# Down-projection of a gated MLP by seven block products: operand sums on VectorE, kept in DRAM, the last product by pairs of row blocks

## The chip, the core and the metric

The kernel runs on one core of one Trainium2 chip. The metric is device time in microseconds (us) of one execution, smaller is better. The median of three runs before the change is 3221.31 us (3219.59 to 3222.55).

## The reference

One layer of a streaming encoder on x of 2048 tokens by 1024 channels, all in 32-bit floats: a token-mixing sublayer, a layer norm, then a gated MLP with a causal convolution, and a second layer norm. What the change touches is the end of it:

```python
def conv_ffn(x, conv_w, conv_b, w_up, w_down):
    h = x @ w_up                                   # 2048 x 1024 by 1024 x 5632
    h = depthwise causal conv, width 3 (h) + conv_b
    gate, val = jnp.split(h, 2, axis=-1)
    return (jax.nn.silu(gate) * val) @ w_down      # 2048 x 2816 by 2816 x 1024
...
x = layer_norm(ALPHA * x + ffn(x), ln2_g, ln2_b)
```

## The kernel before

Every 32-bit product is made of three matrix products of operands split in two: `split` writes the rounded part of a tile with ScalarE (ACT) and the rest, source minus rounded part, with VectorE (DVE); `mm3` issues the three matmuls of 128 by 512 outputs. Both projections of the MLP are done by a seven-product block scheme (two halves in each of the three sizes), so that seven products of half-size blocks replace eight; the price is sums of blocks of the operands and of the results.

**Up-projection** (`ffn_up`, L1714). A loop over 44 steps i (22 pairs of feature columns for the first half of the tokens, then 22 for the second, in reverse) and seven products k in each. A product is 12 matmuls into one PSUM bank of four; `after` adds it into the tiles `pre` on DVE. One step behind, `conv` applies the convolution (ACT, and two DVE operations for each of two parts), the SiLU (ACT) and the product of the two parts, one 128x1024 multiply on GpSimd (POOL); then follows the store `h<-b` into DRAM, issued by SyncE (SP, L1758). `slot_back` (L1656 to L1660) issues the loads `b<-wk` of the split weights of the second half, one per product, also on SP.

**Weight sums for the down-projection** (`down_sums`, L1847), run beside the second half of the up-projection as a background job. For each of 11 row blocks c of w_down it loads a 128x1024 tile `xraw` (one buffer) and two 128x512 tiles `xtmp` (four buffers), makes four differences with `sub`, each 128x512 and on POOL, and stores four tiles `wt` into DRAM (L1874 to L1881).

**Down-projection** (`Down`, L245, and `ffn_down`, L1885). Seven products p in the order 0, 4, 3, 5, 2, 6, 1. The first six have 11 steps c; a step multiplies one token tile (128 features by 1024 tokens, eight row blocks of 128) with one 128x512 weight tile: 8 x 3 = 24 matmuls, into eight PSUM banks, four of which are halves of two two-bank tiles. For each step ahead of the matmuls, `Down.load` (three steps ahead) issues the loads on SP, `Down.sum` (two steps ahead) makes the token sum on POOL for the products 4, 3, 5 and 6 (128x1024, add or subtract) and keeps those of 4 and 3 in DRAM (`hs`), and `Down.split` (one step ahead) splits tokens and weights. After the last step of a product, `after` moves each row block's bank into the result tiles R0 and R1 with ACT (products 0 and 4) or DVE, and makes two more sums of results on POOL. Product 1 goes in three passes over the 11 steps, of four, two and two row blocks, with the split weights kept.

**Last layer norm.** When product 2 is done, the eight row blocks of R1 are final and are queued for `norm_stages`, kind "AP": sums of the rows on ACT, a power on POOL, small operations on DVE, the scale on ACT, the gain on POOL and the shift on DVE. The blocks of R0 follow in product 1 with gain and shift folded into two DVE operations of 128x1024. The residual x is added by `residual`, one DVE operation of 128x1024 for each block, in products 2 (R1) and 6 (R0). `turn` runs after each step and issues stores two steps after they were asked for, on SP's queue.

The order of instructions on each engine is made when the kernel is built, by a scheduler that takes what is ready, first come first; each engine and SP's queue then keep that order. An instruction that waits holds everything behind it on its engine.

Of the kernel before, what the change touches and what calls it, by code (L numbers as in the profile page):

```python
# [15 lines left out]
OP = mybir.AluOpType  # L16
# [228 lines left out]
class Down:  # L245
# [4 lines left out]

    def __init__(self, k):
        self.k, self.half = k, NF // 2
        self.seq = [(p, c, 0, 8) for p in (0, 4, 3, 5, 2, 6) for c in range(self.half)]
        self.seq += [(1, c, a, b) for a, b in ((0, 4), (4, 6), (6, 8)) for c in range(self.half)]
        self.raw, self.ready, self.kept = {}, {}, {}

    def sources(self, p, c):
# [3 lines left out]
        tokens = {0: (h(0, 0),), 4: (h(1, 0), h(1, 1)), 3: (k.d_hs[0][c], h(0, 0)), 5: (h(0, 0), h(1, 0)),  # L261
                  2: (h(1, 1),), 6: (h(0, 1), k.d_hs[1][c]), 1: (h(0, 1),)}[p]
# [7 lines left out]
    def load(self, j):  # L270
        if j >= len(self.seq):
            return
        p, c, a, b = self.seq[j]
        nc = self.k.nc
        tokens, weights = self.sources(p, c)
        x = []
        for d in tokens:
            t = self.k.T([P, (b - a) * P])
            nc.sync.dma_start(t, d[:, a * P:b * P])
            x.append(t)  # L280
        w = None
# [3 lines left out]
        self.raw[j] = x, w  # L285

    def sum(self, j):

        if j >= len(self.seq):
            return  # L290
        p, c = self.seq[j][:2]
        x = self.raw[j][0]
        if len(x) == 2:
            self.k.nc.gpsimd.tensor_tensor(x[0], x[0], x[1], op=OP.add if p == 4 else OP.subtract)
            x.pop()
        if p in (3, 4):
            self.k.store(self.k.d_hs[0 if p == 4 else 1][c], x[0])

    def split(self, j):
        if j >= len(self.seq):  # L300
            return
        p, c, a, b = self.seq[j]
# [8 lines left out]
        self.ready[j] = v, self.k.split_new(x)  # L311

# [4 lines left out]
class Kern:  # L317
# [156 lines left out]
    def setup(self):  # L474
# [27 lines left out]
        self.d_hs = [[self.DT([P, 2 * G], name="hs") for _ in range(NF // 2)] for _ in range(2)]  # L502
# [1211 lines left out]
    def ffn_up(self):  # L1714
# [54 lines left out]
        for i in range(2 * NF):  # L1769
# [30 lines left out]
            for k in range(7):  # L1800
# [46 lines left out]
    def down_sums(self):  # L1847
# [5 lines left out]
        sub = lambda out, x, y: nc.gpsimd.tensor_tensor(out, x, y, op=OP.subtract)  # L1853
# [31 lines left out]
    def ffn_down(self):  # L1885
# [6 lines left out]
        def norm(b, y, kind):  # L1892
            def gen():
                act = kind[0] == "A"
                gain, shift = (nc.gpsimd, nc.vector) if kind[1] == "P" else (None, None)
                yield from self.norm_stages(y, gb, act, gain, shift, self.out[0, b * P:(b + 1) * P, :])
# [15 lines left out]

        def after(k, i, ps):
# [4 lines left out]
            add = nc.vector.tensor_tensor  # L1918
# [140 lines left out]
```

## Time and profile before

| | us |
|---|---|
| median of 3 runs | 3221.31 |
| the profiled execution, its own time | 3227.53 |
| its span (first to last instruction) | 3225.7 |
| outside the span | 1.8 |
| TensorE busy | 3053.4 (95%) |
| VectorE busy | 2474.6 (77%) |
| ScalarE busy | 1595.9 (49%) |
| GpSimd busy | 876.1 (27%) |

Mean granted clock of TensorE is 0.979 of full speed. Names in rows: PE is TensorE (PEld its weight loads), DVE VectorE, ACT ScalarE, POOL GpSimd, SPq the queue of SyncE, which issues nearly all DMAs. A row of a timeline has the start, the time it took, the engine, the operation, output and inputs by tile names (`p` PSUM, `b` a 4 KB tile of the large pool, `m` a 2 KB tile), and in brackets how long the engine stood idle before it and what ended that. Most instructions stand under one line, L133, since a helper records them; they are told apart by tiles.

### The profile page before, as it was taken

Reading aid. Unit: us, or ns where it says so; the run is one execution under the profiler, and the core shown is the slowest. Engines: PE = TensorE matmul, PEld = TensorE weight load, DVE = VectorE, ACT = ScalarE, POOL = GpSimd, SP = SyncE. Lnnn points to the kernel's source line nnn. Section 1 sums busy time; section 2 is a strip of 40 time slices with the busy share of each in tenths; the row PEclk is TensorE's granted clock in tenths of the full one; section 3 lists DMA queues with packets and bytes.
Section 4 is the critical chain, followed back from the end, with each engine's and each line's share of the span. In section 5 each row is a group of like instructions: output and inputs, shape, how many; then the busy total and the mean of one; then the engine's idle time right before and its main releaser. Section 6 shows DMA issues by size and latency. Waiting matters only on the chain. (4 is left out here: it accounts for less than half of the span.)

```text
span 3225.7 us, 44051 instructions
## 1 busy us (share of the span) xinstructions
PE 3053.4 (95%) x14750; PEld 2542.7 (79%) x14750; DVE 2474.6 (77%) x4622; ACT 1595.9 (49%) x3048; POOL 876.1 (27%) x704
## 2 busy tenths in 40 slices
PE   8988899999999999599999999999999999999978
PEld 8886688888888788488787878888777788888866
DVE  5589987987799989988775688999954555568775
ACT  3365746874578777577611244444522322333253
POOL 2017510010010221001222234555433111355441
PEclk9999899999999999899999999999999999999989
DMA  7657784765377332221454777888877766778762
GB/s 251 236 183 279 252 319 150 264 220 200 129 261 256 116 103 66 67 96 53 144 202 173 239 277 287 297 297 294 306 271 290 284 221 216 279 259 339 257 214 90
DMA packets 321089, 704.36 MB, mean 218 GB/s; under 512 B 26906, under 2 KB 128990, under 8 KB 320862
## 3 DMA queue, kind: packets, MB, share of 16 engines
q1 hardware_dynamic: 312222, 685.80, 60.3%
q10 hardware_dynamic: 8640, 15.73, 1.3%
q8 instruction: 117, 1.92, 0.2%
q14 instruction: 110, 0.90, 0.1%
HBM read 449.09 MB, written 252.35 MB: 217 GB/s over the span
## 5 line engine op out<-in xcount | busy, mean ns | idle before, releaser
L133 PE MATMUL p<-b,b 128*128 128x512 f32 (+3 forms) x12568 | 2834.4, 382 | 126.4 <-DVE b L133 53.5
L133 PEld LDWEIGHTS p<-b,b 128*128 128x128 f32 x12568 | 2260.8, 190 | 572.1 <-DVE b L133 55.8
L133 POOL TENSOR_TENSOR b<-b,b 128x1024 f32<-128x1024 f32 (+4 forms) x154 | 386.8, 2516 | 454.3 <-DVE b L133 254.5
L133 ACT ACTIVATE b<-p 128x512 fp32r<-128x512 f32 (+11 forms) x634 | 360.2, 603 | 300.1 <-PE p L133 289.8
L133 DVE TENSOR_TENSOR b<-p,b 128x512 f32<-128x512 f32 (+3 forms) x614 | 388.1, 654 | 139.1 <-PE p L133 93.2
L133 ACT ACTIVATE m<-b,F 128x448 bf16<-128x448 f32 (+3 forms) x448 | 366.2, 820 | 87.1 <-DVE F L133 69.5
L133 ACT ACTIVATE b<-b 128x512 fp32r<-128x512 f32 (+3 forms) x299 | 236.0, 807 | 343.9 <-DVE b L133 118.8
L133 DVE TENSOR_SCALAR_CACHE_REDUCE m<-b,F 128x512 bf16<-128x512 f32 (+6 forms) x476 | 370.1, 808 | 2.4 <-DMA gm<-m 1.6
L133 DVE SCALAR_TENSOR_TENSOR b<-b,cw,b 128x1023 f32<-128x1023 f32 (+1 forms) x176 | 249.2, 1425 | 136.1 <-ACT b L133 135.3
L133 DVE TENSOR_TENSOR b<-b,b 128x1024 fp32r<-128x1024 f32 (+6 forms) x221 | 283.5, 1292 | 56.5 <-ACT b L133 39.3
L133 ACT ACTIVATE b<-m 128x512 fp32r<-128x512 f32 x215 | 133.0, 627 | 285.2 <-DVE m L133 125.0
L133 DVE TENSOR_TENSOR b<-m,b 128x512 fp32r<-128x512 f32 x215 | 203.1, 953 | 83.9 <-ACT b L133 83.7
L133 ACT ACTIVATE b<-b,cw 128x1024 f32<-128x1024 f32 x88 | 107.8, 1238 | 300.0 <-DVE b L133 209.0
L133 ACT ACTIVATE b<-b,mx 128x1024 f32<-128x1024 f32 (+2 forms) x192 | 171.6, 896 | 74.2 <-DVE mx L133 72.4
L133 PE MATMUL p<-ident,b 128*128 128x128 f32 x1248 | 194.9, 275 | 9.5 <-DVE b L133 7.2
L133 DVE SCALAR_TENSOR_TENSOR b<-b,ws,b 128x768 f32<-128x768 f32 (+5 forms) x154 | 154.8, 1034 | 51.6 <-ACT b L133 49.4
L133 DVE CUSTOM_DVE_ANT_0 b<-p,b 128x1024 f32<-128x1024 f32 (+2 forms) x192 | 173.6, 906 | 21.1 <-PE p L133 20.2
L133 PEld LDWEIGHTS p<-ident,b 128*128 128x128 f32 x1248 | 152.8, 141 | 43.0 <-DVE b L133 4.9
L133 PE MATMUL p<-kst,b 128*128 128x384 f32 (+3 forms) x656 | 152.8, 365 | 6.8 <-DVE b L133 4.7
L133 POOL TENSOR_SCALAR b<-b 128x1024 fp32r<-128x1024 f32 (+2 forms) x50 | 53.3, 1069 | 350.3 <-DMA b<-in_w_in_dram 175.2
L133 ACT ACTIVATE m<-p 128x512 f32<-128x512 f32 (+2 forms) x172 | 100.8, 586 | 76.6 <-PE p L133 71.0
L133 PEld LDWEIGHTS p<-kst,b 128*128 128x128 f32 x656 | 114.3, 193 | 28.5 <-ACT b L133 13.5
(127 smaller groups left out, 1663.6 us busy)
## 6 DMA issues: line engine op xcount, KB each, us to landing
b<-wk SPq DMA_DIRECT2D x339, 512.0 KB
wk<-b SPq DMA_DIRECT2D x211, 512.0 KB
b<-h SPq DMA_DIRECT2D x88, 512.0 KB
b<-in_w_ffn_up_dram SPq DMA_DIRECT2D x44, 512.0 KB
h<-b SPq DMA_DIRECT2D x44, 512.0 KB
b<-vv SPq DMA_DIRECT2D x80, 256.0 KB
xT<-b SPq DMA_DIRECT2D x32, 512.0 KB
b<-xT SPq DMA_DIRECT2D x32, 512.0 KB
```

What stands on the lines that cost most here:

```text
L133: return f(*args, **kw)
```

## The change

Token sums: the sum for product 4 is made during product 0 (and the first two steps of 4), spread by the table `early`, and stored in `hs`; product 4 loads it, and makes the sum for product 3 from it in `split`; product 3 makes the one for product 6; each is stored in DRAM. Products 4 and 3 walk their steps in reverse. Only product 5 still sums in `sum`. All these sums, `sub` of `down_sums` and the result sums are on DVE (`nc.vector`). Loads run four steps ahead, sums three, splits two. All norms take the form with gain and shift on DVE; residuals of both halves are added in product 2. Product 1 goes in four passes of two row blocks; the matmuls of row block 7 are held back and issued after all others.

```diff
         self.seq = [(p, c, 0, 8) for p in (0, 4, 3, 5, 2, 6) for c in range(self.half)]
-        self.seq += [(1, c, a, b) for a, b in ((0, 4), (4, 6), (6, 8)) for c in range(self.half)]
+        self.seq += [(1, c, a, a + 2) for a in range(0, 8, 2) for c in range(self.half)]
+        self.early = {n * 4 // 3: self.half - 1 - n for n in range(self.half)}
+    def step(self, j):
+        p, c, a, b = self.seq[j]
+        return p, self.half - 1 - c if p in (3, 4) else c, a, b
...
-        tokens = {0: (h(0, 0),), 4: (h(1, 0), h(1, 1)), 3: (k.d_hs[0][c], h(0, 0)), 5: (h(0, 0), h(1, 0)),
-                  2: (h(1, 1),), 6: (h(0, 1), k.d_hs[1][c]), 1: (h(0, 1),)}[p]
+        tokens = {0: (h(0, 0),), 4: (k.d_hs[0][c],), 3: (k.d_hs[1][c],), 5: (h(0, 0), h(1, 0)), 2: (h(1, 1),),
+                  6: (k.d_hs[2][c],), 1: (h(0, 1),)}[p]
...
+        e = self.early.get(j)
+        side = []
+        if e is not None:
+            side += [get(self.k.d_h[1][e], 0, 8), get(self.k.d_h[1][half + e], 0, 8)]
+        if p == 4:
+            side.append(get(self.k.d_h[0][c]))
+        elif p == 3:
+            side.append(get(self.k.d_h[0][half + c]))
...
     def sum(self, j):
         if len(x) == 2:
-            self.k.nc.gpsimd.tensor_tensor(x[0], x[0], x[1], op=OP.add if p == 4 else OP.subtract)
+            self.k.nc.vector.tensor_tensor(x[0], x[0], x[1], op=OP.subtract)
             x.pop()
-        if p in (3, 4):
-            self.k.store(self.k.d_hs[0 if p == 4 else 1][c], x[0])
...
     def split(self, j):
         self.ready[j] = v, self.k.split_new(x)
+        side = self.side.pop(j, ())
+        add = self.k.nc.vector.tensor_tensor
+        if len(side) > 1:
+            t = side[0]
+            add(t, t, side[1], op=OP.add)
+            self.k.store(self.k.d_hs[0][self.early[j]], t)
+        if p == 4:
+            t = side[-1]
+            add(t, x, t, op=OP.subtract)
+            self.k.store(self.k.d_hs[1][c], t)
+        elif p == 3:
+            t = side[-1]
+            add(t, t, x, op=OP.subtract)
+            self.k.store(self.k.d_hs[2][c], t)
...
-                    if 2 <= k < 5:
-                        down.load(k - 2)
-                    if k == 6:
-                        down.split(0)
+                    if 1 <= k < 5:
+                        down.load(k - 1)
+                    if k > 4:
+                        down.split(k - 5)
...
-        sub = lambda out, x, y: nc.gpsimd.tensor_tensor(out, x, y, op=OP.subtract)
+        sub = lambda out, x, y: nc.vector.tensor_tensor(out, x, y, op=OP.subtract)
...
             elif k == 4:
-                nc.gpsimd.tensor_tensor(R0[i][:, hi], R0[i][:, lo], R1[i][:, lo], op=OP.add)
+                add(R0[i][:, hi], ps, R0[i][:, lo], op=OP.add)
...
-                nc.gpsimd.tensor_tensor(R1[i][:, lo], R1[i][:, hi], R1[i][:, lo], op=OP.subtract)
...
-                queue.append(norm(8 + i, R1[i], "AP"))
+                queue.append(norm(8 + i, R1[i], True))
...
-                elif b0 == 0:
-                    banks = {i: self.PS1() for i in range(4)}
                 else:
-                    t = self.PS2()
-                    banks = {b0: t[:, lo], b0 + 1: t[:, hi]}
+                    banks = {i: self.PS1() for i in range(b0, b1)}
...
-            down.load(j + 3)
-            down.sum(j + 2)
-            down.split(j + 1)
+            down.load(j + 4)
+            down.sum(j + 3)
+            down.split(j + 2)
...
+            if k == 2:
+                if 1 <= c < 9:
+                    load_residual(c - 1)
+                    load_residual(8 + c - 1)
+                if c < 4:
+                    for i in (2 * c, 2 * c + 1):
+                        add(R1[i][:, lo], R1[i][:, hi], R1[i][:, lo], op=OP.subtract)
+                if c >= 3:
+                    residual(c - 3, R0[c - 3])
+                    residual(8 + c - 3, R1[c - 3])
...
+            for i in range(b0, b1):
+                if i == 7 and k == 1:
+                    last.append((i, c, w, xh, xl))
+                else:
+                    pair(i, c, w, xh, xl)
-            norm_tick(k == 1 and (b0 or c % 2 == 0) or c % 2 == 1)
+            norm_tick(k != 1 or c % 3 == 0)
+        for args in last:
+            pair(*args)
```

## Rows read from the trace of the kernel before

**Rows 1.** Waits of PE from 3040 us to the end: total us, times, longest.

```profile
PE p L133 <- DVE b L133: 25.3, 5, 21.5
```

**Rows 2.** Timeline of PE, end of the down-projection.

```profile
3062.01 59.67 PE L133 MATMUL p<-b,b 128*128 128x512 f32 x262 [0.44 <-DVE b L133]
3143.16 51.23 PE L133 MATMUL p<-b,b 128*128 128x512 f32 x215 [21.48 <-DVE b L133]
...
3213.39 0.98 PE L133 MATMUL p<-b,b 128*128 128x512 f32 x3 [0.78 <-DVE b L133]
```

**Rows 3.** Timeline of DVE in products 2 and 6: splits, and evictions (b<-p).

```profile
3060.12 1.23 DVE L133 TENSOR_TENSOR b<-b,b 128x1024 fp32r<-128x1024 f32 x1 [0.58 <-ACT b L133]
3061.27 4.91 DVE L133 TENSOR_TENSOR b<-p,b 128x512 f32<-128x512 f32 x8
...
3095.15 2.48 DVE L133 TENSOR_TENSOR b<-m,b 128x512 fp32r<-128x512 f32 x1 [0.75 <-ACT b L133]
...
3108.56 0.68 DVE L133 TENSOR_TENSOR b<-m,b 128x512 fp32r<-128x512 f32 x1
...
3142.43 1.87 DVE L133 TENSOR_TENSOR b<-p,b 128x512 f32<-128x512 f32 x3
```

**Rows 4.** Windows: length; busy PE, PEld, DVE, ACT, POOL; PEclk; DMA share; GB/s.

```profile
3061.00:3122.00 61.00, 60.23 (x265) 49.25 (x263) 49.34 (x72) 33.90 (x51) 30.50 (x16) 1.00 0.70 235
...
3143.00:3148.00 5.00, 4.84 (x12) 3.83 (x13) 3.28 (x6) 0.63 (x1) 0.00 (x0) 0.51 0.48 146
```

**Rows 5.** Groups by form from 2780 us to the end: count, busy us, mean ns, idle before.

```profile
L133 POOL TENSOR_TENSOR b<-b,b 128x1024 f32<-128x1024 f32 x53 | 151.4, 2861 | 129.4 <-DMA b<-h 59.0 <-PE p L133 22.1 <-DVE b L133 17.8
...
L133 DVE SCALAR_TENSOR_TENSOR b<-b,b 128x1024 f32<-128x1024 f32 x16 | 24.5, 1539 | 6.4 <-DMA b<-x 6.3
...
L133 DVE TENSOR_TENSOR b<-b,b 128x256 fp32r<-128x256 f32 x22 | 8.9, 421 | 18.1 <-ACT b L133 15.6 <-PE p L133 2.3 <-issue 0.2
```

**Rows 6.** Windows of the up-projection, columns as in rows 4.

```profile
2450.00:2500.00 50.00, 46.31 (x203) 37.63 (x203) 19.70 (x24) 12.63 (x21) 20.44 (x14) 1.00 0.75 274
2500.00:2550.00 50.00, 43.99 (x192) 35.50 (x191) 27.52 (x33) 15.85 (x29) 12.26 (x7) 1.00 0.84 310
```

**Rows 7.** Timeline of POOL there: first weight differences of two blocks, the multiply between.

```profile
2447.97 1.29 POOL L133 TENSOR_TENSOR xtmp<-xraw 128x512 f32<-128x512 f32 x1 [14.18 <-DMA xraw<-in_w_ffn_down_dram]
...
2453.19 2.40 POOL L133 TENSOR_TENSOR b<-b,b 128x1024 f32<-128x1024 f32 x1
2469.19 1.30 POOL L133 TENSOR_TENSOR xtmp<-xraw 128x512 f32<-128x512 f32 x1 [13.60 <-DMA xraw<-in_w_ffn_down_dram]
```

**Rows 8.** SP's queue: its waits from 2340 to 2780 us, then its timeline.

```profile
SPq L1758 <- POOL b L133: 157.7, 22, 11.2
...
2455.62 0.32 SPq L1758 DMA_DIRECT2D h<-b  x1
...
2461.11 0.55 SPq L1860 DMA_DIRECT2D xraw<-in_w_ffn_down_dram  x1
```

**Rows 9.** Timeline of ACT: first eviction of product 0, and of product 4.

```profile
2819.55 0.60 ACT L133 ACTIVATE b<-p 128x512 f32<-128x512 f32 x1 [18.84 <-PE p L133]
...
2879.66 0.60 ACT L133 ACTIVATE b<-p 128x512 f32<-128x512 f32 x1 [26.30 <-PE p L133]
```

**Rows 10.** Timeline of DVE in product 1: first and fourth of four norms in a row.

```profile
3180.49 1.28 DVE L133 SCALAR_TENSOR_TENSOR b<-b,nm,b 128x1024 f32<-128x1024 f32 x1
...
3192.28 1.28 DVE L133 SCALAR_TENSOR_TENSOR b<-b,nm,b 128x1024 f32<-128x1024 f32 x1
```

**Rows 11.** A window with the DMA engines full, columns as in rows 4.

```profile
2900.00:2950.00 50.00, 50.00 (x222) 41.09 (x221) 39.16 (x28) 18.75 (x24) 32.91 (x13) 1.00 1.00 396
```

**Rows 12.** Timeline of DVE in an up-projection step without weight differences.

```profile
2604.00 0.69 DVE L133 TENSOR_TENSOR b<-p,m 128x512 f32<-128x512 f32 x1 [0.84 <-PE p L133]
...
2615.96 2.60 DVE L133 SCALAR_TENSOR_TENSOR b<-b,cw,b 128x1023 f32<-128x1023 f32 x2 [3.11 <-ACT b L133]
```

**Rows 13.** Timeline of DVE: its last instruction.

```profile
3220.68 1.28 DVE L133 SCALAR_TENSOR_TENSOR b<-b,nr,b 128x1024 f32<-128x1024 f32 x1
```

More of the change, by code (lines that the diff above doesn't have):

```diff
@@ L272, in load, with get @@
             return
-        p, c, a, b = self.seq[j]
-        nc = self.k.nc
-        tokens, weights = self.sources(p, c)
[L276 to L281, printed above, removed]
+        p, c, a, b = self.step(j)
+        nc, half = self.k.nc, self.half
+        def get(d, x=a, y=b):
+            t = self.k.T([P, (y - x) * P])
+            nc.sync.dma_start(t, d[:, x * P:y * P])
+            return t
+        tokens, weights = self.sources(p, c)
+        x, w = [get(d) for d in tokens], None
         if a == 0:
@@ L285, in load @@
         self.raw[j] = x, w
+        e = self.early.get(j)
[6 more added lines that the diff above has]
+            side.append(get(self.k.d_h[0][half + c]))
+        if side:
+            self.side[j] = side
     def sum(self, j):
@@ L301, in split @@
             return
-        p, c, a, b = self.seq[j]
+        p, c, a, b = self.step(j)
         (x,), w = self.raw.pop(j)
@@ L501, in setup @@
         self.d_wt = [[self.DT([P, 512], name="wt") for _ in range(NF // 2)] for _ in range(4)]
-        self.d_hs = [[self.DT([P, 2 * G], name="hs") for _ in range(NF // 2)] for _ in range(2)]
+        self.d_hs = [[self.DT([P, 2 * G], name="hs") for _ in range(NF // 2)] for _ in range(3)]
         self.I = {}
@@ L1890, in ffn_down, with norm @@
         queue, norming, gb, xs = [], [], None, {}
-        def norm(b, y, kind):
+        def norm(b, y, act):
             def gen():
-                act = kind[0] == "A"
-                gain, shift = (nc.gpsimd, nc.vector) if kind[1] == "P" else (None, None)
-                yield from self.norm_stages(y, gb, act, gain, shift, self.out[0, b * P:(b + 1) * P, :])
+                yield from self.norm_stages(y, gb, act, None, None, self.out[0, b * P:(b + 1) * P, :])
             return gen()
@@ L1911, in residual @@
             nc.vector.scalar_tensor_tensor(y, xs.pop(b), ALPHA, y, op0=OP.mult, op1=OP.add)
+        add = nc.vector.tensor_tensor
         def after(k, i, ps):
-            add = nc.vector.tensor_tensor
             if k == 0:
@@ L1929, in after @@
                 add(R1[i][:, hi], ps, R0[i][:, hi], op=OP.add)
-                nc.gpsimd.tensor_tensor(R1[i][:, lo], R1[i][:, hi], R1[i][:, lo], op=OP.subtract)
             elif k == 2:
                 add(R1[i][:, lo], ps, R1[i][:, lo], op=OP.add)
-                queue.append(norm(8 + i, R1[i], "AP"))
+                queue.append(norm(8 + i, R1[i], True))
                 R1[i] = None
-            elif k == 6:
-                add(R0[i][:, hi], ps, R0[i][:, hi], op=OP.add)
             else:
                 add(R0[i][:, lo], ps, R0[i][:, lo], op=OP.add)
-                queue.append(norm(i, R0[i], "D-" if i >= 6 else "A-"))
+                queue.append(norm(i, R0[i], i < 6))
                 R0[i] = None
+        last = []
         for j, (k, c, b0, b1) in enumerate(down.seq):
             if c == 0:
-                banks = {}
                 if k != 1:
```

17 lines of the change are left out of this document (6 added, 11 removed).

## The prediction, made before the changed kernel was run

> **What bounds the kernel now.** I read the page first: PE is busy 95% of the span, so a gain has to come from the other 5% or from the end. The waits of PE in the last 190 us name DVE for 25.3 us, 21.5 of it in one piece [rows 1]. The timeline of PE shows where: product 6 runs without a gap, then PE stands for 21.48 us [rows 2]. It resumes at 3143.16, and the first eviction of product 6 on DVE runs from 3142.43 to 3143.11 [rows 3]: row blocks 0 and 1 share a two-bank PSUM tile, so block 1's last matmuls wait for block 0's eviction, and that eviction stood in DVE's queue behind 21 us of other work. DVE was busy 49.34 of 61 us in product 6 [rows 4], but many of its instructions were long: the 128x512 split remainder takes 0.68 us alone, and 2.48 us where a POOL operation runs beside it [rows 3]; POOL's 128x1024 operations take 2.86 us each, 53 of them in this stretch [rows 5]. After the stall the clock was granted at 0.51, the lower of its two levels (1.2 of 2.4 GHz), for 5 us, in which 12 matmuls ran [rows 4]. Then I looked for other gaps. Only the up-projection has some: 3.69 and 6.01 us in two windows of 50 us, 9.7 in all [rows 6]. There POOL stands 14 us for the load `xraw` before its first weight difference, and the multiply, ready long before, stands behind it [rows 7]; SP's store `h<-b` waits for that multiply (157.7 us in 22 waits), and the next `xraw` load stands behind the store, 5.5 us later [rows 8]. This ring takes 21.2 us (2447.97 to 2469.19 [rows 7]). A step of the up-projection needs 7 x 12 matmuls; one matmul takes 0.2277 us (60.11 us between the first evictions of products 0 and 4, 264 matmuls [rows 9]), so 19.1 us. The ring is 2.1 us slower than PE, and once the slack is gone PE loses that much a step.
>
> **The change, part by part.** PE's work stays: seven products of 264 matmuls.
>
> *Work taken off POOL in the down-projection.* POOL keeps only the small power. Product 6's DVE work then is: 8 evictions of 0.61 us [rows 3] 4.9; 11 splits of 0.68 + 1.23 [rows 3] 21.0; 8 norms of 3.5 us each (three norms with three 128x256 splits take 11.79 us [rows 10], a split 0.42 [rows 5]) 28.1. That is 54.0 of 60.1 us. It fits, so the eviction that ended the long stall comes in time: **-21.5 us**, and the slow clock goes with it: 5 us hold 22 matmuls at full clock and held 12, **-2.3**. The other waits of rows 1 come to 25.3 - 21.5 = **-3.8**.
>
> *What DVE takes over before that.* Token sums, 33 x 1.23 = 41 us over four products, at most 1.23 to 2.5 a step beside 1.91 of splits, in steps of 5.46 us; evictions in product 4 and result differences, 16 x 0.69. Product 2 is the fullest: splits 21.0, evictions 4.9, differences 5.4, 16 residuals of 1.28 (the like operation in rows 10) to 1.54 [rows 5], 20.5 to 24.6, together 52 to 56 of 60.1. All this lies beside PE, with splits now two steps (10.9 us) ahead; if that cover goes, DVE bounds (rival B). At the ends of five products PE meets DVE's queue; the one such wait of before that shows its size is 0.44 us [rows 2]: bounds 0 and, were DVE a 128x1024 operation and an eviction late, 1.9; I take 0.44 x 5 = **+2.2**, since DVE is less loaded than there.
>
> *Loads, stores and SP.* Per c one load and one store of 512 KB more, 22 DMAs, at 0.32 to 0.55 us of SP each [rows 8], hidden in 360 us. Product 0 is the tightest: 7 steps' own loads, 4 steps of product 4's, 8 pairs for the sums and 8 or 9 stores are 23.6 MB in 60.1 us, 393 GB/s. The trace has 396 GB/s with the DMA engines full and PE without a gap [rows 11], so I take nothing; loads lead by four steps, 21.8 us.
> The Trainium skill's "DMA: Bandwidth & Descriptors" (section "Where 436 GB/s comes from") says that for transfers between HBM and SBUF about 358 GB/s bind. Rows 11 go against it, on a core alone; by it, product 0 would need 66 us, late by 6.
>
> *Weight differences on DVE.* 44 x 0.68 = 30 us, in a stretch where DVE was busy 19.7 to 27.5 of 50 us [rows 6]. What matters is the ring. In a step, DVE works without a gap through convolution and first evictions, and only then idles: 0.84 us before the eviction at 2604.00, 3.11 before the next convolution [rows 12]. The scheduler gives an engine to what is ready, first come first, and the differences come later in the code; so I expect them in those gaps, behind the convolution. POOL's multiply and the store `h<-b` are then no longer behind a difference, and the ring is open: **-9.7**. Bounds: 0 if the ring closes through DVE, and worse if DVE waits long (rivals A and C).
>
> *Product 1.* Steps of 6 matmuls, 1.37 us. DVE needs 0.68 + 0.42 = 1.1 us of splits in the first pass. In a later pass of 15.0 us it needs 11 x 0.42, two norms of 3.5 and two evictions of 0.69: 13.0. In the last, block 6 alone takes 7.5 us of PE, and DVE's 13.0 less the 2.7 us of lead stick out by 2.8; block 7 then runs from splits long made. I take **+4** for the passes; bounds 0 and, if each of the six norms holds up the splits by its own 3.5 us less 2.7 of lead, 5 more than the 2.8.
>
> *The end.* From the last matmul's end, 3214.37 [rows 2], to the span's end 11.3 us: 7.6 of DVE with two norms mixed [rows 13], then 3.7 for the store. With block 6 done before, one norm is left: an eviction, two operations of 1.28, small ones and the power's wait; bounds 5 and 7.6, I take 6.2: **-1.4**.
>
> The sum: -21.5 - 2.3 - 3.8 - 9.7 - 1.4 + 2.2 + 4 = **-32.5**. The profiled execution took 3227.5, so 3195.0 for one like it. The median of the runs, 3221.3, lies 6.2 below it; if part of that is the profile's own cost and part lay in the stalls that go, half of it, 3, stays: 3192, so I forecast **3191**, with 3184 to 3199 of its own.
>
> **Rivals.**
> A, *the ring closes again through DVE*: if differences stand ahead of the convolution in DVE's queue, landing, one or two differences, the convolution's second part with evictions, the multiply and the 5.5 us of SP make about 21 us as before. Against it: rows 12. For it: POOL's order of before put them ahead of the multiply [rows 7]. The 9.7 us stay: **3201**.
> B, *DVE becomes the bound*: 54 of 60.1 us leaves 10%; each split also waits for ACT, 0.58 to 0.75 us [rows 3], twice in a step: 11 x 1.3 = 14 us in products 2 and 6 each, which then need 66 to 70. The lead of 10.9 us takes most; 6 us of each stick out: **3203**. The norms' 3.5 us hold their waits already, which speaks against it. The Trainium skill's "Perfetto Trace Analysis" (section "Optimizing Scalar/DVE Operations") says that if DVE is saturated, moving some work to GPSIMD may make sense, while noting that the two share a port; this change goes the other way. By the first half of that rule product 6 gets slower, and this rival is it; rows 3, 2.48 against 0.68 us, side with the second half.
> C, *slower: DVE waits for the weight rows*. The loads `xraw` keep POOL standing 13.6 to 14.2 us [rows 7]. Should DVE stand as long for each of 11 blocks, evictions stop: PE has four banks, about three products or 8.2 us, and loses 6 us a block, some 8 times, while the ring stays: 3191 + 9.7 + 48 = **3249**. It decides for slower from about 3.4 us lost in each of 11 blocks. Against it: DVE's queue has 10 us of other work in a step, which POOL had not.
> D, *the change does not reach its end in product 0*: at the DMA limit, loads come late beyond the lead; 330 GB/s instead of 393 would put them 11 us back, half the lead, so it shows only as a few us at the next ends: **3195**.
>
> **How the numbers follow.** Chances: the forecast 0.52, A 0.16, B 0.14, D 0.04, C 0.14, of which 0.05 are mild cases that eat just the gain. The range reaches from 3178 (all stalls gone, no price in product 1, the whole 6.2 us) to 3213 (A and B together); it leaves out C. A measurement here can tell 0.2%, 6.4 us, from no change. Faster by more: 0.86 less 0.01 for an A and B that add up with a price of product 1, 0.85; within it 0.05; slower 0.10.
>
> **What the profile would show.** Right: no gap of PE over 2 us at the end of product 6, clock 1.00 there; 128x512 split remainders at 0.68 us; the windows of rows 6 at 50 of 50; SP's wait of L1758 near nothing; one norm after the last matmul. Wrong: PE waits named DVE in the up-projection, or `DMA xraw` as what DVE waited for (A, C); DVE without a gap in products 2 and 6 with PE waiting at their ends (B); DMA full and PE waiting in product 0 or 4 (D).

## The result, and the profile after

The median after the change is 3177.57 us (3175.19 to 3179.14, four runs), against 3221.93 (3219.59 to 3222.62) before, where a fourth run has joined the three ahead of the prediction: a ratio of 0.9859, interval [0.9847, 0.9871], 44.4 us faster. The forecast was 3191 with a range from 3178: the direction was right and the main mechanism in part, the size was too small, and the median lies 0.4 us under the range. The profiled execution took 3178.85 us (span 3177.1, mean granted clock 0.986 against 0.979). Line numbers of the kernel after are 29 higher in the parts quoted: L1787 is the store `h<-b`.

To see where the 48.6 us between the two spans lie, I cut each at two places. The first is the start of the last eight transposes of operands, which stand before anything that the change touches; the timelines of PE have them, first before, then after:

```profile
2243.49 1.03 PE L133 MATMUL p<-ident,xraw 128*128 128x128 f32 x8
```

```profile
2238.74 1.03 PE L133 MATMUL p<-ident,xraw 128*128 128x128 f32 x8
```

So 4.7 us were won before the change could act; over twenty profiles of kernels alike up to there the place moves between 2231.4 and 2244.8. The second cut is the first eviction of product 0 on ACT, before in [rows 9], here in the timeline of ACT after:

```profile
2798.11 0.60 ACT L133 ACTIVATE b<-p 128x512 f32<-128x512 f32 x1 [9.84 <-PE p L133]
```

**Stretch A**, between the cuts (the second half of the up-projection), went from 576.1 to 559.4: -16.7. **Stretch B**, from there to the span's end, from 406.2 to 378.9: -27.3 (to the first eviction of product 2 nothing, 241.7 against 241.5; the rest lies behind it).

Stretch B first. The timeline of PE after (columns as in rows 2):

```profile
2801.94 60.25 PE L133 MATMUL p<-b,b 128*128 128x512 f32 x264 [0.69 <-ACT b L133]
2863.60 291.17 PE L133 MATMUL p<-b,b 128*128 128x512 f32 x1281 [1.41 <-DVE b L133]
3156.19 0.73 PE L133 MATMUL p<-b,b 128*128 128x512 f32 x2 [1.41 <-ACT b L133]
3157.28 3.15 PE L133 MATMUL p<-b,b 128*128 128x512 f32 x11 [0.36 <-DVE nt L133]
3161.32 6.87 PE L133 MATMUL p<-b,b 128*128 128x512 f32 x29 [0.89 <-DVE nt L133]
```

From 2863.60 PE runs 291 us without a stop: the 21.48 us of [rows 2] are gone. The waits of PE after, from 3020 us to the end (columns as in rows 1):

```profile
PE p L133 <- ACT b L133: 1.4, 1, 1.4
PE p L133 <- DVE nt L133: 1.3, 2, 0.9
```

Of the 25.3 us that PE waited for `DVE b` there [rows 1] no row is left. The windows after (columns as in rows 4; the product windows reach over parts of products 0, 4, 2 and 6):

```profile
2250.00:2300.00 50.00, 47.97 (x209) 38.57 (x208) 45.97 (x55) 19.95 (x33) 22.16 (x12) 1.00 0.84 298
2300.00:2350.00 50.00, 45.81 (x191) 36.52 (x190) 47.24 (x64) 27.73 (x47) 4.79 (x2) 0.97 0.80 276
2350.00:2400.00 50.00, 50.00 (x222) 41.40 (x221) 36.38 (x43) 12.81 (x24) 7.18 (x3) 1.00 0.93 334
2450.00:2500.00 50.00, 50.00 (x222) 41.42 (x221) 32.24 (x41) 13.95 (x24) 6.68 (x3) 1.00 0.91 320
2500.00:2550.00 50.00, 50.00 (x223) 41.39 (x222) 31.56 (x39) 13.98 (x27) 7.21 (x3) 1.00 0.78 284
2741.00:2798.00 57.00, 57.00 (x253) 47.19 (x252) 42.19 (x41) 20.70 (x29) 2.70 (x1) 1.00 1.03 411
2798.00:2858.00 60.00, 59.31 (x262) 48.53 (x261) 35.03 (x36) 21.29 (x30) 0.00 (x0) 1.00 1.00 403
2980.00:3040.00 60.00, 60.00 (x266) 49.44 (x265) 48.98 (x56) 17.86 (x22) 0.00 (x0) 1.00 0.69 246
3040.00:3100.00 60.00, 60.00 (x266) 49.40 (x265) 46.23 (x93) 35.45 (x62) 9.21 (x8) 1.00 0.58 188
```

The two windows of [rows 6] now hold 50.00 of 50 us of PE. But stretch A gained more than these two windows had lost. Windows before, for a part of it that the prediction had not looked at:

```profile
2250.00:2300.00 50.00, 46.58 (x197) 37.74 (x197) 45.56 (x47) 20.31 (x32) 30.58 (x17) 0.97 0.81 289
2300.00:2350.00 50.00, 43.34 (x181) 34.51 (x180) 45.91 (x58) 25.66 (x43) 17.77 (x10) 0.96 0.80 283
2350.00:2400.00 50.00, 50.00 (x217) 41.26 (x216) 28.27 (x35) 17.10 (x30) 17.29 (x11) 0.97 0.82 288
```

The granted clock is 0.97, 0.96 and 0.97 here, so for some of the time it was at the lower of its two levels. The timeline of PE before, in the same part:

```profile
2261.78 19.34 PE L133 MATMUL p<-b,b 128*128 128x512 f32 x84 [0.91 <-DVE b L133]
2283.63 34.84 PE L133 MATMUL p<-b,b 128*128 128x512 f32 x144 [2.51 <-DVE b L133]
2319.68 3.01 PE L133 MATMUL p<-b,b 128*128 128x512 f32 x12 [1.21 <-DVE b L133]
2325.74 20.71 PE L133 MATMUL p<-b,b 128*128 128x512 f32 x84 [3.05 <-DVE b L133]
2348.84 1.76 PE L133 MATMUL p<-b,b 128*128 128x512 f32 x4 [2.39 <-DVE b L133]
```

Five waits for DVE, 10.07 us, and by the windows some 0.10 x 50 = 5 us of clock. After, the same part has waits of 0.97, 0.98, 0.40, 1.70 and 1.96, 6.01 us, and 0.03 x 50 = 1.5 us of clock. That is 9.7 (ring) + 4.1 (gaps) + 3.5 (clock) = 17.3, against 16.7 measured.

### The profile page after: what moved, and what is told of

Read it like the earlier page. It is cut to its first block, busy times and chain, and to the rows that moved or that the text cites. A ratio compares the mean times of both kernels' runs of the same rounds, so it can differ in the third digit from the quotient of the medians.

```text
span 3177.1 us, 44106 instructions
## 1 busy us (share of the span) xinstructions
PE 3042.5 (96%) x14750; PEld 2534.0 (80%) x14750; DVE 2486.0 (78%) x4737; ACT 1587.3 (50%) x3051; POOL 644.4 (20%) x592
## 5 line engine op out<-in xcount | busy, mean ns | idle before, releaser
L133 DVE TENSOR_TENSOR b<-b,b 128x1024 fp32r<-128x1024 f32 (+6 forms) x268 | 302.9, 1141 | 76.0 <-DMA b<-h 29.9
L133 POOL TENSOR_TENSOR b<-b,b 128x1024 f32<-128x1024 f32 (+3 forms) x94 | 226.8, 2415 | 493.1 <-DVE b L133 339.8
L133 DVE TENSOR_TENSOR b<-m,b 128x512 fp32r<-128x512 f32 x215 | 151.2, 711 | 49.0 <-ACT b L133 48.8
```

What stands on the lines that cost most here:

```text
L133: return f(*args, **kw)
```

## The experiments

Each kernel was timed beside the kernel before on one chip, and its ratio is to that; the medians of before were 3224.1, 3223.2, 3227.4, 3219.9 and 3222.0 in the five groups (3221.9 beside after itself), so ratios compare across groups and medians do not. Stretches A and B of each profile:

| kernel | ratio, 95% | A | B |
|---|---|---|---|
| before | 1 | 576.1 | 406.2 |
| b_again | one run | 576.9 | 408.4 |
| b_diff_dve | 0.9942 [0.9929, 0.9954] | 557.1 | 406.8 |
| b_hstore | 1.0001 [0.9992, 1.001] | 581.3 | 405.5 |
| b_sum_dve | 0.9985 [0.9975, 0.9995] | 578.3 | 400.0 |
| b_norm_dve | 0.9957 [0.9943, 0.997] | 576.1 | 392.1 |
| b_norm_res | 0.9947 [0.9931, 0.9964] | 576.9 | 392.6 |
| b_min | 0.9897 [0.9882, 0.9911] | 558.6 | 391.9 |
| b_min_sum | 0.9866 [0.9848, 0.9884] | 557.3 | 381.3 |
| after | 0.9859 [0.9847, 0.9871] | 559.4 | 378.9 |
| a_diff_pool | 0.9923 [0.991, 0.9937] | 577.2 | 379.4 |
| a_sum_pool | 0.9868 [0.9853, 0.9883] | 559.2 | 378.8 |
| a_split1 | 0.9871 [0.9855, 0.9887] | 562.5 | 379.0 |
| a_norm_pool | 0.9875 [0.9858, 0.9893] | 559.2 | 385.1 |
| a_p1_old | 0.9863 [0.9847, 0.9879] | 558.6 | 383.0 |
| a_p1_old2 | 0.9876 [0.9859, 0.9893] | 559.5 | 383.4 |
| a_again | 0.9859 [0.9844, 0.9873] | 558.7 | 379.2 |
| best1 | 0.9849 [0.983, 0.9869] | 557.8 | 378.3 |
| best2 | 0.9852 [0.983, 0.9874] | 557.2 | 377.3 |
| a_again2 | 0.9858 [0.984, 0.9877] | 558.8 | 378.7 |

### The weight differences

b_diff_dve is before with one line changed, a_diff_pool is after with it undone, and b_again is before, unchanged:

```diff
-        sub = lambda out, x, y: nc.gpsimd.tensor_tensor(out, x, y, op=OP.subtract)
+        sub = lambda out, x, y: nc.vector.tensor_tensor(out, x, y, op=OP.subtract)
```

> The kernel before with one edit: the weight differences of the down-projection on VectorE. Between the two profiles the up-projection's second half and the step into it gained 16.7 us (first eviction of product 0 came 21.4 us earlier, the last transposes before it 4.7 us earlier). Theory 1: all of that comes from this edit, 9.7 us from the ring through POOL's queue (gaps in the windows 2450 to 2550 go) and the rest from DVE no longer slowed by POOL between 2261 and 2349 us: 3205 us. Theory 2: the differences only account for the ring, the rest comes from elsewhere in the change: 3212 us.

> The changed kernel with the weight differences back on POOL, all else as changed. Theory 1: it gives back what they brought, 16.7 us: 3194 us, with PE gaps of 1.3 to 2.5 us a step again in the windows 2450 to 2550. Theory 2: it gives back the ring alone, 9.7 us: 3187 us.

> The kernel before once more, for a second profile of it. The first took 6.2 us more than the median, and stood 4.7 us behind the changed kernel's before the first instruction that the change touches. If that is chance of one execution, this one stands elsewhere (3219 to 3223 us, and the same place earlier by some us); if the profile costs it, it repeats (3227 us).

b_diff_dve took 3205.93 us (3201.09 to 3209.09), 18.2 under before, as theory 1 had it: the line alone is the whole gain of stretch A, and stretch B with its long stall stays. From 2342 us to 2780, where the window ends, its timeline of PE has no gap, so the gaps of [rows 6] are gone too:

```profile
2342.19 438.17 PE L133 MATMUL p<-b,b 128*128 128x512 f32 x1932 [0.56 <-DVE b L133]
```

a_diff_pool took 3199.03 (3195.1 to 3202.27), and A goes back to 577.2. That is theory 1's direction, 5 us above its 3194; the stretches account for 18.3 us of the difference to after, and the rest is within the intervals of the two ratios. b_again (3231.86, one run) came out above both of its expectations, with the transposes at 2244.81; it repeats both stretches of before within 2.2 us. What the line does to DVE between 2250 and 2350 us, by groups by form (columns as in rows 5), before and then in b_diff_dve:

```profile
L133 DVE SCALAR_TENSOR_TENSOR b<-b,cw,b 128x1022 f32<-128x1022 f32 x10 | 15.2, 1524 | 0.1
...
L133 DVE TENSOR_TENSOR b<-p,b 128x512 f32<-128x512 f32 x20 | 13.1, 678 | 0.0
L133 DVE TENSOR_TENSOR b<-m,b 128x512 fp32r<-128x512 f32 x12 | 11.8, 999 | 1.8 <-ACT b L133 1.8
```

```profile
L133 DVE TENSOR_TENSOR b<-p,b 128x512 f32<-128x512 f32 x25 | 16.3, 677 | 0.0
...
L133 DVE SCALAR_TENSOR_TENSOR b<-b,cw,b 128x1022 f32<-128x1022 f32 x9 | 11.5, 1274 | 0.0
...
L133 DVE TENSOR_TENSOR b<-m,b 128x512 fp32r<-128x512 f32 x12 | 7.9, 681 | 0.7 <-ACT b L133 0.6
```

DVE is 45.6 of 50 us busy there, and takes on differences of 0.68 us and more; but this part of its convolution comes down from 1524 to 1274 ns and these splits from 999 to 681, as POOL has less to do beside them (before 30.58 and 17.77 us in the two windows, in b_diff_dve 23.57 and 5.80). The evictions, with one operand in PSUM, stay at 678 and 677. A form that meets what is left on POOL is no shorter: the 128x512 splits `b<-b,b` take 1422 and 1423. The Trainium skill's "GPSIMD Engine Reference" (section "1. Specifications") says that the two engines contend over their SBUF interfaces, among others where a DVE instruction has two SBUF inputs. These rows agree: the two forms with two SBUF inputs change, the one with a PSUM input does not.

**Is it the ring?** b_hstore opens the link that the prediction named, SP waiting with `h<-b` for POOL's multiply:

```diff
+                nc.scalar.dma_start(self.d_h[hf][f], a[0])
```

(in place of the same store on SP's queue.)

> The kernel before with one edit: the store of each up-projection step is issued from ScalarE's queue instead of SyncE's; the weight differences stay on POOL. This opens the ring at another place (the load xraw no longer stands behind that store). If the ring is the cause of the gaps of 9.7 us, they go and the gaps between 2261 and 2349 stay: 3212 us, unless ScalarE, which now waits for POOL's multiply, takes some back. If POOL's mere presence beside DVE is the cause, nothing changes: 3222 us.

It took 3224.0: no change, and A is 5.2 us longer than before. PE still has gaps, as its timeline shows (two of five rows between 2410 and 2500 us):

```profile
2433.76 20.84 PE L133 MATMUL p<-b,b 128*128 128x512 f32 x84 [2.14 <-DMA b<-wk]
2456.07 19.33 PE L133 MATMUL p<-b,b 128*128 128x512 f32 x84 [1.46 <-DMA b<-wk]
```

All five now name the loads of weights `b<-wk`, as two of the five did before; they come to 7.9 us against 9.7. The waits of POOL in b_hstore from 2340 to 2780 us:

```profile
POOL xtmp L133 <- DMA xtmp<-in_w_ffn_down_dram: 51.5, 6, 11.4
```

In before POOL had waited 97.9 us for `xraw` and 0.5 for `xtmp`; here 27.6 are left for `xraw`. And the waits of SP's queue there:

```profile
SPq L1877 <- POOL xtmp L133: 54.0, 7, 8.5
```

The ring closed at another link: SP's stores `wt` (L1877) now wait 54 us for POOL's differences, where they waited 6.8 before, loads `b<-wk` stand behind them, and POOL waits for `xtmp`, whose loads SP issues behind those stores and loads. So opening the one link that the prediction named is not enough; with the differences on DVE, in b_diff_dve, the gaps are gone.

### What removed the 21.5 us

Two single parts of the change, done alone in before:

```diff
 b_sum_dve, in Down.sum
-            self.k.nc.gpsimd.tensor_tensor(x[0], x[0], x[1], ...
+            self.k.nc.vector.tensor_tensor(x[0], x[0], x[1], ...
 b_norm_dve, in the function after(), k == 2
-                queue.append(norm(8 + i, R1[i], "AP"))
+                queue.append(norm(8 + i, R1[i], "A-"))
```

> Before, with the 128x1024 token sums of products 4, 3, 5 and 6 on VectorE and nothing else changed. Theory 1 (in product 6 VectorE falls behind because GpSimd's 128x1024 operations lengthen its own instructions): 11 of the 16 GpSimd operations of product 6 go, so the 21.5 us stall at its end shrinks to under 10 us though VectorE gets 13.5 us more work; about 3210 us against 3222 to 3224 for before. Theory 2 (VectorE falls behind because of the amount of work and the short lead of one step): 11 x 1.23 us more work, so the stall grows to 25 to 35 us: 3226 to 3236.

> Before, with the norms of R1 in the form with gain and shift in two VectorE operations of 128x1024, so that GpSimd's gain goes and VectorE's work hardly changes; the token sums stay on GpSimd. Theory 1 (overlap with GpSimd lengthens VectorE's instructions): 8 of the GpSimd operations from product 6 go, the stall at its end shrinks, to 8 to 16 us: 3210 to 3218. Theory 2 (amount and lead): the stall stays within 3 us of 21.5: 3222 to 3224. Theory 3 (the eviction stands in VectorE's queue behind a norm that waits for GpSimd's gain, a wait and no length): the stall goes nearly whole, under 5 us: 3203 to 3207.

They took 3217.49 us and 3208.42. What is left of the stall, in the timeline of PE of b_sum_dve and of b_norm_dve:

```profile
3132.50 50.67 PE L133 MATMUL p<-b,b 128*128 128x512 f32 x215 [16.02 <-DVE b L133]
```

```profile
3119.64 51.67 PE L133 MATMUL p<-b,b 128*128 128x512 f32 x215 [7.52 <-DVE b L133]
```

b_sum_dve gives DVE 13.5 us more to do in products 2 and 6, and the stall shrinks, from 21.48 to 16.02: theory 2 (the amount of work) fails by its sign, theory 1 by its size, since only a quarter goes. The gain and shift of the norms count for more: 7.52 are left, between theory 1 (8 to 16, POOL lengthens DVE) and theory 3 (under 5, DVE stands for POOL's gain). Both are at work, as DVE's groups by form show from the eviction of product 2 to that of product 6. Behind the last bar stands how long DVE was idle before them, and for what: `nr` is POOL's small power in a norm, `b` its gain. First before, then b_sum_dve, then b_norm_dve:

```profile
L133 DVE TENSOR_TENSOR b<-b,b 128x1024 f32<-128x1024 f32 x8 | 14.1, 1766 | 5.0 <-POOL b L133 5.0
...
L133 DVE SCALAR_TENSOR_TENSOR nt<-nr,nv 128x1 f32<-128x1 f32 x8 | 3.9, 484 | 6.3 <-POOL nr L133 6.3
```

```profile
L133 DVE SCALAR_TENSOR_TENSOR nt<-nr,nv 128x1 f32<-128x1 f32 x8 | 3.9, 486 | 3.5 <-POOL nr L133 3.5
```

```profile
L133 DVE SCALAR_TENSOR_TENSOR nt<-nr,nv 128x1 f32<-128x1 f32 x8 | 3.9, 483 | 2.6 <-POOL nr L133 2.6
```

DVE stood 11.3 us for POOL's results before, 3.5 in b_sum_dve and 2.6 in b_norm_dve. Its own instructions ran longer than the same forms alone by some 18, 16 and 9 us in the same stretch (an estimate from the traces: nine, eight and four instructions were held). So b_sum_dve gained mostly by shorter waits for POOL, and b_norm_dve by both. DVE and POOL before, in the stall, show what an overlap costs. First the timeline of DVE:

```profile
3133.14 0.16 DVE L133 TENSOR_TENSOR nr<-nr,nt 128x1 f32<-128x1 f32 x1
3133.34 2.35 DVE L133 TENSOR_TENSOR nmr<-nm,nr 128x1 f32<-128x1 f32 x1
```

Two instructions alike in shape, one fifteen times as long. The timeline of POOL at that time:

```profile
3133.33 2.34 POOL L133 TENSOR_TENSOR b<-b,b 128x1024 f32<-128x1024 f32 x1 [0.66 <-ACT b L133]
```

The instruction of one column that meets POOL's gain starts and ends with it.

Then on from b_norm_dve: b_norm_res also loads and adds the residuals of R0 in product 2, b_min is that with `sub` on DVE, b_min_sum that with the token sums on DVE at their old places.

```diff
 b_norm_res
-            if k in (2, 6):
-                half = 8 if k == 2 else 0
...
-                    load_residual(half + c - 1)
...
-                    residual(half + c - 3, (R1 if half else R0)[c - 3])
+            if k == 2:
...
+                    load_residual(c - 1)
+                    load_residual(8 + c - 1)
...
+                    residual(c - 3, R0[c - 3])
+                    residual(8 + c - 3, R1[c - 3])
```

> Before, with the R1 norms' gain and shift on VectorE as in b_norm_dve (3208, a stall of 7.5 us left at the end of product 6) and besides the eight residuals of R0 moved from product 6 to product 2. Theory 1 (what is left of the stall is plain amount: residuals and norms together fill VectorE in product 6): 8 x 1.22 = 9.8 us less there, the stall falls under 2 us, 3200 to 3204. Theory 2 (the work only moves): product 2 gets 9.8 us more and the wait appears at its end instead, 3 to 8 us: 3205 to 3209.

> b_norm_res with the weight differences on VectorE too: three small edits of before; token sums on GpSimd, sums two and splits one step ahead, product 1 in its three passes and no second copy in DRAM stay. Theory 1 (gains of the two stretches add: 17 to 18 us from the up-projection and 20 to 23 from product 6): 3181 to 3186, so that 4 to 8 us are left for the rest of the change. Theory 2 (sums on VectorE and the longer lead are needed once VectorE has the rest): a stall of 5 to 10 us at the end of product 2 or 6 stays: 3188 to 3195.

> b_min with the token sums on VectorE, made at the old places (product 6's sums in products 2 and 6), nothing more. Theory 1 (the sums on GpSimd lengthen VectorE's splits in products 2 and 6, mean 1150 ns against 687 in after, and that makes the 5.2 and 2.3 us waits at their ends): splits come down to about 0.7 us, which gives back 26 x 0.46 + 34 x 0.25 = 20 us of VectorE time for 14 us of sums; both waits fall under 2 us; 4 to 8 us faster than b_min, 0.987 to 0.9885 of before. Theory 2 (product 6's sums must leave products 2 and 6 altogether, which is what the DRAM copy is for): waits stay or grow, 5 to 10 us at either end; 0.989 to 0.991 of before.

b_norm_res took 3209.43 us, 0.9947 of before against 0.9957 without the move: theory 2 holds, the wait only moved. The timeline of PE has 5.26 at the end of product 2 and 2.42 at the end of product 6, where b_norm_dve had 0.23 and 7.52:

```profile
3058.76 62.04 PE L133 MATMUL p<-b,b 128*128 128x512 f32 x266 [5.26 <-DVE b L133]
3123.21 50.41 PE L133 MATMUL p<-b,b 128*128 128x512 f32 x214 [2.42 <-DVE b L133]
```

b_min took 3193.43: A and B add, and B keeps the 7.5 us of waits, as theory 2 said, though what it names as needed is two things. b_min_sum (3177.16, 0.9866 against 0.9897) parts them: moving the sums' engine alone removes both waits, with neither the DRAM copies nor the lead. Its timeline of PE runs through the ends of products 2 and 6:

```profile
2759.77 382.81 PE L133 MATMUL p<-b,b 128*128 128x512 f32 x1684
```

DVE's groups by form in products 2 and 6, of b_min and then of b_min_sum:

```profile
L133 DVE TENSOR_TENSOR b<-m,b 128x512 fp32r<-128x512 f32 x26 | 29.9, 1150 | 2.1 <-ACT b L133 2.1
L133 DVE TENSOR_TENSOR b<-b,b 128x1024 fp32r<-128x1024 f32 x18 | 26.8, 1489 | 1.6 <-ACT b L133 1.1 <-issue 0.5
```

```profile
L133 DVE TENSOR_TENSOR b<-b,b 128x1024 fp32r<-128x1024 f32 x17 | 20.7, 1218 | 1.3 <-ACT b L133 1.3
L133 DVE TENSOR_TENSOR b<-m,b 128x512 fp32r<-128x512 f32 x26 | 18.9, 727 | 1.7 <-ACT b L133 1.5
L133 DVE TENSOR_TENSOR b<-b,b 128x1024 f32<-128x1024 f32 x11 | 13.4, 1219 | 0.9 <-DMA b<-hs 0.9
```

DVE takes on 13.4 us of sums and spends 29.9 + 26.8 - 18.9 - 20.7 = 17.1 us less on its splits (1.2 of it is a split that falls outside the window). The gain over b_min, 0.0031 of 3222 or 10 us, is larger than theory 1 expected.

### Parts undone in after

a_sum_pool puts the sums back on POOL (in the new places), a_split1 takes the lead back to two steps for sums and one for splits, a_norm_pool gives the norms of R1 back the form with gain on POOL, a_p1_old puts product 1 back into three passes without the held-back block.

```diff
 a_sum_pool
-            self.k.nc.vector.tensor_tensor(x[0], x[0], x[1], op=OP.subtract)
+            self.k.nc.gpsimd.tensor_tensor(x[0], x[0], x[1], op=OP.subtract)
...
-        add = self.k.nc.vector.tensor_tensor
+        add = self.k.nc.gpsimd.tensor_tensor
 a_split1
-                    if k > 4:
-                        down.split(k - 5)
+                    if k > 5:
+                        down.split(k - 6)
...
-            down.sum(j + 3)
-            down.split(j + 2)
+            down.sum(j + 2)
+            down.split(j + 1)
 a_norm_pool
-... self.norm_stages(y, gb, act, None, None, ...
+... self.norm_stages(y, gb, act, *((nc.gpsimd, nc.vector) if b >= 8 else (None, None)), ...
 a_p1_old
-... for a in range(0, 8, 2) for c in range(self.half)]
+... for a, b in ((0, 4), (4, 6), (6, 8)) for c in range(self.half)]
...
-                    banks = {i: self.PS1() for i in range(b0, b1)}
+                    t = [self.PS1() for _ in range(4)] if not b0 else self.PS2()
+                    banks = dict(enumerate(t)) if not b0 else {b0: t[:, lo], b0 + 1: t[:, hi]}
...
-                if i == 7 and k == 1:
+                if False:
...
-            norm_tick(k != 1 or c % 3 == 0)
+            norm_tick(k != 1 or b0 or c % 2 == 0)
```

> After, with all token sums back on GpSimd (the same sums, in the same steps; result sums, weight differences and norms stay on VectorE). They lie in products 0, 4, 3 and 5 and none in product 6. Theory 1 (lengthening matters only where VectorE is nearly full): VectorE gets 41 us less and some longer instructions in products 0 to 5, covered by the lead of two steps; 3176 to 3181, the same as after (3177.6). Theory 2 (GpSimd beside VectorE costs PE wherever it runs): waits of PE for VectorE of 2 us or more at the ends of products 0, 4, 3 or 5: 3183 to 3190.

> After, with the sums two and the splits one step ahead as in before (loads stay four ahead). Theory 1 (the lead hides only what is left once GpSimd's operations are gone from product 6): a few waits of PE for VectorE at ends of products come back, 1 to 3 us each, no long stall; 3181 to 3190. Theory 2 (the lead, not the engine, removed the 21.5 us): a stall of 10 to 20 us at the end of product 6 or 2 comes back: 3190 to 3200.

> After, with the R1 norms back in the form with the scale on ScalarE, the gain on GpSimd and the shift on VectorE. Theory 1 (the norm's form was the main cause of the 21.5 us): VectorE's instructions in product 6 are lengthened again and a stall of 8 to 15 us comes back at its end: 3186 to 3193. Theory 2 (the form hurt only together with the residuals in product 6 and the norms spread over every second step): with these gone and splits two steps ahead the longer instructions are hidden, stall under 2 us: 3177 to 3180.

> After, with product 1 in three passes of four, two and two row blocks, without holding back block 7, and with the old ticks of the norms there. Theory 1 (the pairs and the held-back block are worth the shorter tail, 11.3 against 8.9 us from the last matmul to the end, and the waits in product 1, 4.2 against 2.7): 3180 to 3183. Theory 2 (only the tail counts, or the pairs cost as much as they give): 3176 to 3179.

> a_p1_old again, beside after on the same chip. Theory 1 (pairs and held-back block are worth the shorter tail and fewer waits, 2.4 + 1.5 us): 3 to 5 us above a_again. Theory 2 (worth nothing that can be measured): within 1.5 us of a_again.

> After, unchanged, beside the others on one chip: 0.985 to 0.987 of before (first measured 0.9859).

a_sum_pool took 3178.62 us, the same as after: in the new order no sum stands in product 2 or 6, and in products 0 to 5 DVE has room for longer instructions. So POOL's sums cost nothing that can be measured where DVE is not nearly full; what counts is that products 2 and 6 are free of them, which either the engine (b_min_sum) or the new order (a_sum_pool) brings about. a_split1 took 3180.19 with B at 379.0: no stall came back at the end of product 2 or 6 (new are two waits of 1.75 and 0.73 us, in products 0 and 3), so the lead isn't what removed the stall; theory 2 fails, and theory 1 expected a little more. a_norm_pool took 3187.24 (3178.66 to 3191.16), 0.9875, and a stall is back, between the two theories, at the end of product 6 in its timeline of PE:

```profile
3111.64 55.39 PE L133 MATMUL p<-b,b 128*128 128x512 f32 x236 [4.59 <-DVE b L133]
```

4.59 us, with B 6.2 above after: in this profile the norms' form costs something even with the rest of the change in place, but less than the 14 us that it is worth in before. The profile is that of the slowest of four runs, and the intervals of the ratios overlap, so the price is not well known.

a_p1_old took 3182.27, in theory 1's range, but its ratio, 0.9863, does not tell it from after's 0.9859. a_p1_old2 took 3181.77 beside 3176.44 for a_again, each of its four runs above each of the other's: 5.3 us, theory 1. In B it is 383.0 and 383.4 against 379.2: the tail behind the last matmul is 11.6 instead of 8.9 us, and the waits in product 1 are 4.0 and 3.1 us instead of 2.8.

### A version with fewer edits

best1 is b_min_sum with product 1 and the lead of after, best2 the same with the lead of before (product 1's banks and, in best1, the first loads and splits change with them; left out below). Neither has the sums' new order nor its extra copy in DRAM; results are summed on POOL as before.

```diff
 best1 and best2, on top of b_min_sum
-        self.seq += [(1, c, a, b) for a, b in ((0, 4), (4, 6), (6, 8)) for c in range(self.half)]
+        self.seq += [(1, c, a, a + 2) for a in range(0, 8, 2) for c in range(self.half)]
...
+                if i == 7 and k == 1:
+                    last.append((i, c, w, xh, xl))
...
-            norm_tick(k == 1 and (b0 or c % 2 == 0) or c % 2 == 1)
+            norm_tick(c % 3 == 0 if k == 1 else c % 2 == 1)
 best1 alone
-            down.load(j + 3)
-            down.sum(j + 2)
-            down.split(j + 1)
+            down.load(j + 4)
+            down.sum(j + 3)
+            down.split(j + 2)
```

> b_min_sum with product 1 in four pairs, block 7 held back, and with loads four, sums three and splits two steps ahead as in after. Theory 1 (the pairs' 5 us add, and nothing else of the change is needed): about 5 us under b_min_sum, 3170 to 3174 where after has 3176.4; 0.984 to 0.9853 of before. Theory 2 (in after the pairs pay only because the sums have left product 6): a wait comes back at the end of product 2 or 6, 3176 to 3180.

> best1 with the old leads (loads three, sums two, splits one step ahead). Theory 1 (in product 1 a step of a pair is 1.4 us, less than a split on ScalarE and VectorE in a row takes, so one step of lead is too short): several waits of 0.3 to 1 us in the passes, 2 to 6 us above best1. Theory 2 (the lead is worth nothing, as a_split1 said of the products before): within 1.5 us of best1.

> After, unchanged, beside the others: 0.985 to 0.987 of before.

They took 3173.25 and 3172.95 us, after 3175.97 beside them. The intervals overlap (0.9849 [0.983, 0.9869] and 0.9858 [0.984, 0.9877]), so they are not shown to be faster; they are as fast with a smaller change. best1 lies in the range of its theory 1, with no wait of over 0.63 us at the ends of products 2 and 6. best2 with the short lead loses nothing, against its theory 1.

## Why the prediction was right in direction and short in size

- **-21.5 and -2.3, the stall and its slow clock: right in size, the mechanism only in part.** POOL's operations did lengthen DVE's: b_min_sum gave DVE 13.4 us more work, and its splits alone gave back more than that. But I had nothing for DVE standing still: in product 6 before, it waited 11.3 us for POOL's power and gain, and much of what b_sum_dve and b_norm_dve won is that wait. The change took the sums and the gain off POOL, so that both effects went (DVE's waits for POOL in product 6 came down to 0.4 us), and the size came out all the same; that it did is in part luck. After, 128x512 split remainders in products 2 and 6 take 0.69 us on average, DVE is busy 48.98 and 46.23 of 60 us (I had 52 to 56 and 54), and the clock is 1.00 there.
- **-9.7, the up-projection: the step that failed.** "Only the up-projection has some: 3.69 and 6.01 us in two windows of 50 us, 9.7 in all" left out the first 100 us of the same stretch, where the background differences already ran beside a DVE that was 45 of 50 us busy: 4.1 us of gaps and some 3.5 of clock more. The term measured 16.7 by the profiles, and 18.2 in b_diff_dve. I had applied the lengthening to product 6 and not here. The bounds for this term went from worse to -9.7 and none lay beyond, so the range was cut off at the fast end. Its lower end had no sum behind it either: with all stalls gone, no price in product 1 or at the ends of products, and the whole 6.2 us, the prediction's own terms make 3182.6, not 3178.
- **The ring: partly right.** Its 9.7 us went. But SP's wait for the multiply did not come down to "near nothing": L1758 had 157.7 us in 22 waits [rows 8], L1787 has 117.4 in 22, with no gap of PE beside it. And b_hstore shows that the one link that I named did not make it alone.
- **-3.8 and +4, product 1:** net +0.2 forecast. Before, its waits were 2.40 + 0.81 + 0.24 + 0.78 = 4.2 us; after, 1.41 + 0.36 + 0.89 = 2.7: net -1.5. Whatever the pairs held up of the splits, PE lost nothing by it.
- **-1.4, the end:** the last matmul ends at 3168.2, 8.9 us before the span's end instead of 11.3: -2.4, the right kind and 1.0 more than forecast.
- **+2.2, ends of products:** the waits are there, 0.69 + 1.41 us at the start of products 4 and 3. But the way to product 2's first eviction is no longer than before (241.5 against 241.7), so as much went elsewhere; what went is not shown.
- **Half of the 6.2 us between profile and median: wrong.** The two profiles differ by 4.7 us ahead of the touched code, so the profiled execution before was long in a place that the change leaves alone. Nor does a profile cost time as such: over the 18 other kernels of the table that have more than one run, the profiled execution lies 0.5 us below the median on average. The sum belonged against the median: 3221.3 - 32.5 = 3188.8. The last step, from 3192 to 3191, had no reason given.

Together: 7.0 (up-projection) + 2.2 (offset, 3191 against 3188.8) + 1.7 (product 1) + 1.0 (end) + 2.2 (ends of products) = 14.1, against 3191.0 - 3177.6 = 13.4; the rest is within what one profile can tell.

Rival A did not come: DVE did wait for weight tiles, in its waits from 2330 to 2760 us after,

```profile
DVE xtmp L133 <- DMA xtmp<-in_w_ffn_down_dram: 17.3, 5, 4.6
DVE xtmp L133 <- DMA xraw<-in_w_ffn_down_dram: 3.9, 1, 3.9
```

but with no gap of PE beside it from 2318.59 us on; this is also rival C, whose 13.6 to 14.2 us per block became 4.6 at most. Rival B did not come: the windows leave DVE 11 to 14 us. Behind it stood the rule of the Trainium skill's "Perfetto Trace Analysis" (section "Optimizing Scalar/DVE Operations"), that GpSimd may relieve a full DVE. Its first half did not hold here, where work taken back from GpSimd made the kernel faster (b_min_sum); its second half did, that the shared port may take the gain back. Rival D did not come: product 0 ran at 411 GB/s with the DMA share at 1.03 and PE at 57.00 of 57, product 4 at 403 with 1.00 and 59.31 of 60. The 358 GB/s of the Trainium skill's "DMA: Bandwidth & Descriptors" (section "Where 436 GB/s comes from") did not bind on this core.

Not tried alone: POOL's lengthening of DVE without the waits for its results, the move of the residuals without that of the norms, the norms started every step instead of every second, and the result sums' engine.

## What to carry to other kernels

Before work is given to GpSimd "because VectorE is full", look at the mean time of VectorE's own forms with two SBUF inputs, with and without GpSimd beside them: here 13.4 us of sums taken back made VectorE some 16 us faster on its splits. Look also at how long VectorE stands for GpSimd's results: a step handed to GpSimd in the middle of a chain holds up VectorE's whole queue, 11.3 us in product 6 here. When a cause is found in one stretch, look for the same cause in every window where both engines are busy, and sum the gaps over the whole stretch that an edit touches rather than over the windows where they were first seen. Set the sum of gains against the median when the two profiles differ ahead of the touched code.

## What was not expected of the hardware

- A VectorE instruction of 128x1 with two SBUF inputs can be held as long as one of 128x1024: 2.35 us in place of 0.16, ending with GpSimd's 2.34 us. In product 6 before, three of 24 such instructions of the norms met a GpSimd operation of 128x1024 and took 2.3 us each.
- What counts is who starts first. In the trace of before from 2790 us on, 49 of 50 VectorE instructions with two SBUF inputs that started while GpSimd was at an operation (its small power left aside) were held until that ended and did all their own work then: they ended 0.55 us (128x512), 1.08 (128x1024) or 0.02 (128x1) behind it. The 21 that had begun before GpSimd's operation did took no longer than alone.
- Evictions from PSUM are not held: 678 ns beside GpSimd's differences and 677 with most of them gone.
- The start of the touched stretch moves by up to 13.4 us (2231.4 to 2244.8) between profiles of kernels alike up to there, more than several terms of the sum.
